# State-space stage of a decoder layer: products with the input issued ahead into two kept PSUM banks

## The chip, the cores and the metric

The kernel runs on one core of one Trainium2 chip. The metric is the device time of one execution in microseconds (us), the median of several runs.

## The reference

One layer of a decoder trunk over 1024 tokens and 1024 channels, in float32. Four token mixers of width 256 (a diagonal complex state-space model, two kinds of attention and RWKV-7 time mixing) read the same projection of the input; their outputs are projected up, gated and summed; then follow an output projection, layer norm, an MLP and a gated embedding. The change lies in the state-space mixer. Cut to that:

```python
# 16 groups of 16 channels, 64 complex states each
bu_re = jnp.einsum('bsgh,gph->bsgp', ug, bb_re)
bu_im = jnp.einsum('bsgh,gph->bsgp', ug, bb_im)
_, _, x_re, x_im = lax.associative_scan(combine, (a_re, a_im, bu_re, bu_im), axis=1)
y = (jnp.einsum('bsgp,ghp->bsgh', x_re, c_re) - jnp.einsum('bsgp,ghp->bsgh', x_im, c_im)
     + d * ug)
y = jax.nn.gelu(y.reshape(bsz, s, BRANCH_WIDTH))
y = y * jax.nn.sigmoid(y @ glu_w + glu_b)
```

## The kernel before

**The whole program.** TensorE (PE) does nearly everything as matmuls of 128x128 weights with 512 columns in a fast float32 format, three for each float32-accurate product. They fill two kinds of PSUM banks: three with the tag `mm` (function `pmm`, line 358) and five with the tag `x` (`px`, line 361).

**Who sets the order.** A planner, the class `Driver` (line 89), runs at build time. Each stage is a Python generator; a `yield 0.1` says "go on 0.1 us after my last result is there", by the planner's own table of costs. While a stage waits, the planner takes the next matmuls of a filler, `merges` (line 1647): up-projections and gates of branches that are already there, called the dense work below. The planner thereby fixes the order of instructions of PE; those of DVE and ACT are chained in the order of the planner's start times. So a different cost or yield in one stage moves instructions in everything that is planned behind it.

**The state-space stage** (`s5`, line 1370) works on 128 chunks of 8 tokens. It has two halves (`p4`), each with four state tiles of 128 states, real and imaginary. A half goes through these steps:

1. PE: products of the input `U` with `GT`, 16 of them, into two `x` banks (lines 1387 to 1392).
2. DVE: rotation by `E` into `Z`, eight scans over the chunks, rotation back into `X`, first the real part (`i` = 0), then the imaginary part (lines 1394 to 1414). The two parts are written by one instruction each.
3. PE: for each of two banks (`g4`) four column blocks (`j`): one product of `U` with `Tg` (what a chunk's own input gives; 128 rows), then one of `X` real and one of `X` imaginary with `Hm` (what the state gives; 64 rows, the lower half for `g4` = 0, the upper for `g4` = 1), added up in the same place (lines 1418 to 1426).
4. ACT and DVE: GELU of each bank into `Y` (lines 1427 to 1433); SP stores `Y` (line 1435).

Behind both halves, the stage loads its result as `yt`, multiplies it with the GLU weights `gw` and stores it. These products are in plain float32: one of them appears in the trace as two passes, that is two weight loads and two MATMUL records. In the text, step 3 of a half is a product block.

Lines 327 and 280 in the trace are those of the helpers that issue every matmul and every other instruction, so groups are told apart by the tiles' names.

Of the kernel before, what the change touches and what calls it, by code (L numbers as in the profile page):

```python
# [16 lines left out]
P = 128  # L17
# [299 lines left out]
def body(ctx, tc, I, O, dbg=None):  # L317
    nc = tc.nc
    drv = Driver()
# [23 lines left out]
    def nm(s):  # L343
        uid[0] += 1
        return f"{s}_{uid[0]}"
# [15 lines left out]
    def px():  # L361
        return ps.tile([P, 512], F32, tag="x", name=nm("x"), bufs=5)
# [907 lines left out]
    def s5_tables(pool):  # L1270
# [93 lines left out]
        for k in range(5, 7):  # L1364
            grow(k)
            yield 0.1
        yield from s5(pool, GT, Tg.rearrange("p g s h -> p g (s h)"), Hm.rearrange("p i a s h -> p i a (s h)"),
                      E.rearrange("p i j a -> p i a j"), U)

    def s5(pool, GT_, Tg_, Hm_, E_, U_):  # L1370
        def tt(o, a, b, op):
            V.tensor_tensor(out=o, in0=a, in1=b, op=op)

        def tq():
            return pool.tile([P, 4, P], F32, tag="s2k", name=nm("tq"), bufs=4)

        gw = pool.tile([P, 2, 256], F32, tag="s2k", name="gw", bufs=4)
        SY.dma_start(out=gw, in_=I["glu_w"].rearrange("(a p) c -> p a c", p=P))
        yield 0.1
        for p4 in range(2):  # L1380
            a4 = slice(p4 * 4, p4 * 4 + 4)
            GT, Hm, Ev = GT_[:, :, a4], Hm_[:, :, a4], E_[:, :, a4]
            Tg, U = Tg_[:, p4 * 8:p4 * 8 + 8], U_[:, p4 * 8:p4 * 8 + 8]
            Z = pool.tile([P, 2, 4, P], F32, tag="t1k", name=nm("Z"), bufs=2)
            X = pool.tile([P, 2, 4, P], F32, tag="t1k", name=nm("X"), bufs=2)
            yield 0.1
            sr, si = px(), px()
            for i, o in ((0, sr), (1, si)):
                for j in range(4):
                    for e in range(2):  # L1390
                        T.matmul(o[e * 64:e * 64 + 64, j * P:(j + 1) * P], lhsT=GT[:, i, j, e * 64:e * 64 + 64],
                                 rhs=U[:, j * 2 + e, :], start=True, stop=True)
            s3r, s3i = (o.rearrange("p (a j) -> p a j", j=P) for o in (sr, si))
            a, b = tq(), tq()
            tt(a, s3r, Ev[:, 0], ALU.mult)
            tt(b, s3i, Ev[:, 1], ALU.mult)
            tt(Z[:, 0], a, b, ALU.add)
            a, b = tq(), tq()
            tt(a, s3i, Ev[:, 0], ALU.mult)
            tt(b, s3r, Ev[:, 1], ALU.mult)  # L1400
            tt(Z[:, 1], a, b, ALU.subtract)
            for i in range(2):
                for j in range(4):
                    pr = p4 * 4 + j
                    V.tensor_tensor_scan(out=Z[:, i, j, :], data0=s5k[:, pr:pr + 1].to_broadcast([P, P]),
                                         data1=Z[:, i, j, :], initial=0.0, op0=ALU.mult, op1=ALU.add)
            z3 = [Z[:, i, :, 0:127] for i in range(2)]
            e3 = [Ev[:, i, :, 0:127] for i in range(2)]
            for i in range(2):
                G.memset(X[:, i, :, 0:1], 0.0)  # L1410
                a, b = tq()[:, :, 0:127], tq()[:, :, 0:127]
                tt(a, e3[0], z3[i], ALU.mult)
                tt(b, e3[1], z3[1 - i], ALU.mult)
                tt(X[:, i, :, 1:128], a, b, ALU.subtract if i == 0 else ALU.add)
            Y = pool.tile([P, 8, P], F32, tag="t1k", name=nm("Y"), bufs=2)
            Ye = Y.rearrange("p (a e) c -> p e a c", e=2)
            yield 0.1
            for g4 in range(2):
                o = px()
                for j in range(4):  # L1420
                    g = j * 2 + g4
                    pr, es = g // 2, slice((g % 2) * 64, (g % 2) * 64 + 64)
                    os_ = o[:, j * P:(j + 1) * P]
                    T.matmul(os_, lhsT=Tg[:, g], rhs=U[:, g, :], start=True, stop=False)
                    for i in range(2):
                        T.matmul(os_, lhsT=Hm[es, i, pr], rhs=X[es, i, pr, :], start=False, stop=i == 1)
                w = pool.tile([P, 512], F32, tag="s2k", name=nm("gl"), bufs=4)
                A.activation(out=w, in_=o, func=AF.Square)
                V.tensor_scalar(out=w, in0=w, scalar1=0.044715, scalar2=1.0, op0=ALU.mult, op1=ALU.add)
                tt(w, o, w, ALU.mult)  # L1430
                A.activation(out=w, in_=w, func=AF.Tanh, scale=math.sqrt(2.0 / math.pi))
                V.scalar_tensor_tensor(out=Ye[:, g4], in0=w.rearrange("p (a b) -> p a b", b=P), scalar=1.0,
                                       in1=o.rearrange("p (a b) -> p a b", b=P), op0=ALU.add, op1=ALU.mult)
            for s in range(8):
                SY.dma_start(out=SCR["y"].rearrange("(g h) s c -> s h g c", h=16)[s, :, p4 * 8:p4 * 8 + 8],
                                  in_=Y[s * 16:(s + 1) * 16])
        yt = []
        for i, tg in enumerate(("Tg", "GT")):
            y_ = pool.tile([P, 1024], F32, tag=tg, name=nm("yt"), bufs=1)
            SY.dma_start(out=y_, in_=SCR["y"][i * P:(i + 1) * P].rearrange("p s c -> p (s c)"))  # L1440
            yt.append(y_)
        yield 0.1
        for ct in range(2):
            for h in range(2):
                hs = slice(h * 512, (h + 1) * 512)
                o = px()
                for kt in range(2):
                    T.matmul(o, lhsT=gw[:, kt, ct * P:(ct + 1) * P], rhs=yt[kt][:, hs], start=kt == 0, stop=kt == 1)
                th = pool.tile([P, 512], F32, tag="s2k", name=nm("gl"), bufs=4)
                A.activation(out=th, in_=o, func=AF.Tanh, scale=0.25, bias=s5k[:, 8 + ct:9 + ct])  # L1450
                yf = pool.tile([P, 512], F32, tag="s2k", name=nm("yf"), bufs=4)
                V.scalar_tensor_tensor(out=yf, in0=th, scalar=1.0, in1=yt[ct][:, hs], op0=ALU.add, op1=ALU.mult)
                if h == 0:
                    ynat = pool.tile([P, 1024], F32, tag="a", name=nm("ynat"), bufs=1)
                A.activation(out=ynat.rearrange("p (c s) -> p c s", s=8)[:, :, h * 4:h * 4 + 4],
                             in_=yf.rearrange("p (s c) -> p c s", s=4), func=AF.Copy, scale=0.25)
            SY.dma_start(out=SCR["Y"][0, ct], in_=ynat)
        yield 0.1
        finished["s5"] = True
# [41 lines left out]
    for n in MERGES:  # L1501
        g = MERGES.index(n)
# [748 lines left out]
```

## Time and profile before

| | |
|---|---|
| median of 3 runs | 1860.12 us (1857.07 to 1865.44) |
| the profiled execution | 1853.48 us, span 1851.7 us |
| PE busy | 1802.2 us, 97% of the span |
| DVE busy | 1238.8 us, 67% |
| ACT busy | 715.7 us, 39% |
| POOL busy | 206.7 us, 11% |
| mean granted clock of PE | 0.99 |
| the state-space stage's products | 661.4 to 741 us |

A busy PE is not one at its peak: matmuls overlap, a record's duration is longer than the distance between starts, and at the lower clock PE is busy all the time too. What a step costs on PE is therefore read from the distance of starts, and from the granted clock of a stretch (1.00 is 2.4 GHz, 0.50 is 1.2 GHz).

### The profile page before, as it was taken

How to read it: one execution, taken by the hardware profiler on the slowest of the kernel's cores; microseconds unless marked ns; L12 is line 12 of the kernel's file. 1: busy time of each engine (PE TensorE's matmuls, PEld its weight loads, DVE VectorE, ACT ScalarE, POOL GpSimd, SP SyncE). 2: the span in 40 equal slices, each digit the busy share in tenths (PEclk: the TensorE clock that was granted, in tenths of full speed). 3: DMA queues.
4: the chain of work that ended last, by engine and by line, in shares of the span. 5: the costliest groups of instructions: out<-in, count | busy, mean ns of one | idle time of the engine just before them, and what ended most of it. 6: DMA issues, size and time to landing. Idle time of an engine off the chain costs nothing.

```text
span 1851.7 us, 27604 instructions
## 1 busy us (share of the span) xinstructions
PE 1802.2 (97%) x9651; PEld 1469.5 (79%) x9651; DVE 1238.8 (67%) x2596; ACT 715.7 (39%) x1412; POOL 206.7 (11%) x279
## 2 busy tenths in 40 slices
PE   8999999998999999999999999999999999999998
PEld 7877777777888877777877887788888887888876
DVE  8675855615876665688867667666656666866574
ACT  5443343224554312555544116343333344443230
POOL 0331111110000000000000001111111211122000
PEclk9999999999999989999999999999999999999999
DMA  7344222224432412412154128898888899988441
GB/s 256 106 125 111 75 85 91 69 74 131 139 108 74 101 40 61 141 55 64 45 197 164 53 68 237 243 254 224 250 247 242 212 289 266 281 226 222 127 148 46
DMA packets 178013, 275.27 MB, mean 149 GB/s; under 512 B 37825, under 2 KB 59617, under 8 KB 177745
## 3 DMA queue, kind: packets, MB, share of 16 engines
q1 hardware_dynamic: 155552, 226.31, 37.6%
q0 software_dynamic: 22320, 47.18, 12.9%
q8 instruction: 76, 1.25, 0.3%
q14 instruction: 65, 0.52, 0.1%
HBM read 199.76 MB, written 56.89 MB: 139 GB/s over the span
## 4 chain that ended last, share of the span: by engine, by line
PE 59%; DVE 7%; DMA 3%; ACT 2%; issue 1%; SPq 0%; DVEq 0%; ACTq 0%; POOLq 0%
PE mm L327 29%; PE x L327 29%; DVE R L280 2%; PE x L332 2%; DMA wr<-in_mlp_w2t_dram 1%; DVE W L280 1%; DVE tq L280 1%; DVE sn L280 1%; DMA scr_g<-gs 1%; DMA wl<-in_mlp_w_dram 0%; DVE Z L280 0%; DMA wr<-wl 0%; SPq L280 0%; ACT W L280 0%; ACT R L280 0%
## 5 line engine op out<-in xcount | busy, mean ns | idle before, releaser
L327 PE MATMUL mm<-t,wh 128*128 128x512 f32 x1600 | 511.3, 401 | 2.7 <-ACT th L280 1.4
L327 PEld LDWEIGHTS mm<-t,wh 128*128 128x128 f32 x1600 | 291.8, 189 | 64.4 <-issue 3.8
L327 PE MATMUL mm<-t,wl 128*128 128x512 f32 x800 | 313.5, 392 | 0.4 <-DVE wl L280 0.4
L327 PE MATMUL x<-t,wp 128*128 128x512 f32 x1152 | 267.5, 392 | 6.8 <-ACT wp L280 4.4
L327 PEld LDWEIGHTS x<-t,wp 128*128 128x128 f32 x1152 | 217.5, 189 | 54.2 <-ACT wp L280 5.2
L327 PE MATMUL x<-sx,wp 128*128 128x512 f32 x768 | 179.6, 389 | 0.3 <-DVE wp L280 0.3
L327 PEld LDWEIGHTS mm<-t,wl 128*128 128x128 f32 x800 | 150.8, 189 | 33.8 <-DVE wl L280 0.9
L327 PEld LDWEIGHTS x<-sx,wp 128*128 128x128 f32 x768 | 144.1, 188 | 30.6 <-DVE wp L280 0.7
L280 ACT CAST wh<-wr 128x512 fp32r<-128x512 f32 (+1 forms) x125 | 74.5, 596 | 123.4 <-PE mm L327 92.4
L280 ACT CAST wp<-wr 128x512 fp32r<-128x512 f32 x96 | 59.0, 620 | 143.0 <-DMA wr<-wl 68.7
L280 DVE TENSOR_TENSOR wp<-wr,wp 128x512 fp32r<-128x512 f32 x96 | 65.7, 688 | 71.2 <-ACT wp L280 71.1
L280 POOL TENSOR_TENSOR wl<-wr,wh 128x512 fp32r<-128x512 f32 x50 | 67.4, 1349 | 280.5 <-ACT wh L280 280.3
L327 PE MATMUL mm<-t,wp 128*128 128x512 f32 x384 | 90.2, 390 | 0.0
L327 PE MATMUL mm<-sx,wp 128*128 128x512 f32 x384 | 89.9, 389 | 0.1
L327 PE MATMUL mm<-wo,t 128*128 128x512 f32 x384 | 89.0, 391 | 0.0
L327 PEld LDWEIGHTS mm<-t,wp 128*128 128x128 f32 x384 | 71.9, 188 | 15.7 <-DVE wp L280 0.9
L327 PEld LDWEIGHTS mm<-sx,wp 128*128 128x128 f32 x384 | 72.0, 188 | 15.4 <-DVE sx L280 0.5
L327 PEld LDWEIGHTS mm<-wo,t 128*128 128x128 f32 x384 | 71.6, 188 | 14.5
L280 DVE TENSOR_TENSOR wp<-wl,wp 128x512 fp32r<-128x512 f32 x64 | 43.8, 688 | 42.9 <-ACT wp L280 42.9
L280 DVE TENSOR_TENSOR wl<-wr,wh 128x512 fp32r<-128x512 f32 (+1 forms) x75 | 47.4, 634 | 35.8 <-ACT wh L280 32.9
L280 DVE TENSOR_TENSOR wp<-wh,wp 128x512 fp32r<-128x512 f32 x64 | 43.9, 689 | 29.5 <-ACT wp L280 29.5
L280 ACT CAST wp<-wl 128x512 fp32r<-128x512 f32 x64 | 39.3, 620 | 53.7 <-PE x L327 26.2
(379 smaller groups left out, 3188.1 us busy)
## 6 DMA issues: line engine op xcount, KB each, us to landing
wr<-in_w_in_dram SPq DMA_DIRECT2D x110, 256.0 KB
scr_H<-sn SPq DMA_DIRECT2D x100, 256.0 KB
wr<-in_mlp_w_dram SPq DMA_DIRECT2D x84, 256.0 KB
sn<-scr_H SPq DMA_DIRECT2D x84, 256.0 KB
wh<-in_mlp_w_dram SPq DMA_DIRECT2D x56, 256.0 KB
wl<-in_mlp_w_dram SPq DMA_DIRECT2D x56, 256.0 KB
wr<-wl POOLq DMA_DIRECT2D x32, 256.0 KB, 6.2
wl<-wr POOLq DMA_DIRECT2D x32, 256.0 KB, 4.4
```

Of the source, the lines that this page charges most:

```text
L280: r = f(*a, **kw)
L327: return nc.tensor.matmul(out, lhsT=lhsT, rhs=rhs, **kw)
L332: return nc.tensor.transpose(out, in_, idn)
```

## The change

The `Tg` products move ahead of the step that turns `Z` into `X`: two `x` banks are taken there, eight products are issued into them, and the banks are marked as held for the planner until their last product. Then come the products with `X` real for both banks, a `yield 0.1`, and those with `X` imaginary, each bank followed by its GELU. Since the four column blocks of a bank are now open at the same time, only the first product of a bank carries the start flag.

```diff
+            o2 = [px(), px()]
+
+            def product(g4, j, i):
+                g = j * 2 + g4
+                pr, es = g // 2, slice((g % 2) * 64, (g % 2) * 64 + 64)
+                ab = (Tg[:, g], U[:, g, :]) if i < 0 else (Hm[es, i, pr], X[es, i, pr, :])
+                T.matmul(o2[g4][:, j * P:(j + 1) * P], lhsT=ab[0], rhs=ab[1], start=i < 0 and j == 0, stop=i == 1,
+                         skip_group_check=j > 0)
+            for g4 in range(2):
+                drv.held.add(o2[g4].name)
+                for j in range(4):
+                    product(g4, j, -1)
             z3 = [Z[:, i, :, 0:127] for i in range(2)]
...
             yield 0.1
             for g4 in range(2):
-                o = px()
                 for j in range(4):
-                    g = j * 2 + g4
-                    pr, es = g // 2, slice((g % 2) * 64, (g % 2) * 64 + 64)
-                    os_ = o[:, j * P:(j + 1) * P]
-                    T.matmul(os_, lhsT=Tg[:, g], rhs=U[:, g, :], start=True, stop=False)
-                    for i in range(2):
-                        T.matmul(os_, lhsT=Hm[es, i, pr], rhs=X[es, i, pr, :], start=False, stop=i == 1)
+                    product(g4, j, 0)
+            yield 0.1
+            for g4 in range(2):
+                o = o2[g4]
+                for j in range(4):
+                    product(g4, j, 1)
+                drv.held.discard(o.name)
                 w = pool.tile([P, 512], F32, tag="s2k", name=nm("gl"), bufs=4)
```

PE's order in the first product block before (`x_7263` and `x_7282` are the two banks, `mm_...` is dense work; in the program each bank has four such pairs of rows):

```order
L327 MATMUL mm_7256<-y_6597,vl_7123 128x512
L327 MATMUL x_7263<-U,Tg 128x128
L327 MATMUL x_7263<-X_7147,Hm 128x128 x2
...
L327 MATMUL x_7282<-U,Tg 128x128
L327 MATMUL x_7282<-X_7147,Hm 128x128 x2
...
L327 MATMUL mm_7325<-t_107,wh_7128 128x512
```

48 dense matmuls stand between the products with `GT` and this block.

PE's order of the same half in the change (the banks are now `x_7187` and `x_7188`):

```order
L327 MATMUL x_7151<-U,GT 64x128 x8
L327 MATMUL x_7152<-U,GT 64x128 x8
L327 MATMUL x_7187<-U,Tg 128x128 x4
L327 MATMUL x_7188<-U,Tg 128x128 x4
L327 MATMUL mm_7136<-t_115,wh_7084 128x512
...
L327 MATMUL mm_7257<-y_6571,vl_7123 128x512
L327 MATMUL x_7187<-X_7147,Hm 128x128 x4
L327 MATMUL x_7188<-X_7147,Hm 128x128 x4
L327 MATMUL x_7187<-X_7147,Hm 128x128 x4
L327 MATMUL x_7188<-X_7147,Hm 128x128 x4
L327 MATMUL mm_7257<-y_6597,vh_7122 128x512
```

The `Tg` products have moved right behind `GT`; then 39 dense matmuls (12, 24 and 3) follow and then all 16 `Hm` products, real part first, with no dense work between the two parts. Behind them stand 24 dense matmuls, the second half's `GT` and `Tg`, 39 dense ones (9, 24 and 6) and its `Hm` products.

DVE's order between the first half's imaginary part of `X` and the second half's first rotation, in the change:

```order
L280 TENSOR_TENSOR X_7147<-tq_7204,tq_7205 128x4x127
L280 TENSOR_TENSOR wl_7238<-wr_7030,wh_7237 128x512
L280 TENSOR_SCALAR gl_7273<-gl_7273 128x512
L280 TENSOR_TENSOR gl_7273<-x_7187,gl_7273 128x512
L280 TENSOR_SCALAR gl_7283<-gl_7283 128x512
L280 SCALAR_TENSOR_TENSOR Y_7209<-gl_7273,x_7187 128x4x128
L280 TENSOR_TENSOR gl_7283<-x_7188,gl_7283 128x512
L280 SCALAR_TENSOR_TENSOR th_7222<-th_7222,mm_7257 128x512
L280 SCALAR_TENSOR_TENSOR Y_7209<-gl_7283,x_7188 128x4x128
...
L280 SCALAR_TENSOR_TENSOR th_7255<-th_7255,mm_7304 128x512
...
L280 TENSOR_TENSOR tq_7359<-x_7341,E 128x512
```

Both GELUs (`gl`, `Y`) are now interleaved; before, the first bank's three instructions stood ahead of the second's. The number of instructions in between is the same, 13.

Further on, the planner's times differ and so does the order of the second attention: behind its last product with the values, 39 dense matmuls (27 and 12) stand before the next gate, where there were 15 (3 and 12). On SP the first load of `yt` stands ahead of three loads of weights that it stood behind.

## Rows read from the trace of the kernel before

**Rows 1.** The page, part 1: engine, busy time, share of the span, instructions.

```profile
PE 1802.2 (97%) x9651; PEld 1469.5 (79%) x9651; DVE 1238.8 (67%) x2596; ACT 715.7 (39%) x1412; POOL 206.7 (11%) x279
```

**Rows 2.** Windows around the state-space stage, by engine, with granted clock and DMA share.

```profile
core 0: us, PE busy (x) PEld busy (x) DVE busy (x) ACT busy (x) POOL busy (x), PEclk, DMA share, GB/s
674.30:679.00 4.70, 3.35 (x20) 2.43 (x18) 3.89 (x6) 0.00 (x0) 0.00 (x0) 1.00 0.10 28
679.00:688.30 9.30, 9.30 (x31) 7.07 (x30) 1.81 (x3) 1.23 (x2) 0.00 (x0) 0.50 0.00 0
688.30:692.40 4.10, 4.10 (x11) 3.21 (x11) 2.88 (x6) 2.04 (x4) 0.00 (x0) 0.50 0.16 47
...
707.50:717.50 10.00, 8.60 (x49) 6.50 (x48) 8.00 (x13) 1.23 (x2) 0.00 (x0) 1.00 0.21 66
```

**Rows 3.** Timeline, first product block: start, us, engine, instruction [idle before <-releaser].

```profile
672.92 0.69 DVE L280 TENSOR_TENSOR X<-tq,tq 128x508 f32<-128x508 f32 x1
...
674.34 0.38 PE L327 MATMUL x<-U,Tg 128*128 128x128 f32 x2
...
675.65 0.69 DVE L280 TENSOR_TENSOR X<-tq,tq 128x508 f32<-128x508 f32 x1
...
676.48 0.46 PE L327 MATMUL x<-X,Hm 64*128 64x128 f32 x2 [1.35 <-DVE X L280]
...
677.29 0.71 PE L327 MATMUL x<-X,Hm 64*128 64x128 f32 x4
...
677.92 0.49 PE L327 MATMUL x<-U,Tg 128*128 128x128 f32 x2
...
678.34 0.71 PE L327 MATMUL x<-X,Hm 64*128 64x128 f32 x4
```

**Rows 4.** Timeline, second product block: the gap, and one bank's square and product to Y.

```profile
709.76 0.46 PE L327 MATMUL x<-X,Hm 64*128 64x128 f32 x2 [1.40 <-DVE X L280]
...
713.42 0.60 ACT L280 ACTIVATE gl<-x 128x512 f32<-128x512 f32 x1 [6.27 <-PE x L327]
...
715.97 0.69 DVE L280 SCALAR_TENSOR_TENSOR Y<-gl,x 128x512 f32<-128x512 f32 x1 [0.70 <-ACT gl L280]
```

**Rows 5.** PE timeline elsewhere: 260-column passes, alternating 64-row products, products with GT.

```profile
66.18 0.28 PE L327 MATMUL x<-vl,t 128*128 128x260 f32 x1
...
66.53 0.28 PE L327 MATMUL x<-vl,t 128*128 128x260 f32 x1
...
93.11 2.82 PE L327 MATMUL x<-AR,BK 64*128 64x128 f32 x32
...
661.42 1.97 PE L327 MATMUL x<-U,GT 128*64 128x128 f32 x32
...
663.32 0.73 PE L327 MATMUL mm<-t,wh 128*128 128x512 f32 x2
```

**Rows 6.** Windows where the state-space tables are made; columns as in rows 2.

```profile
624.40:627.80 3.40, 3.40 (x32) 3.36 (x32) 0.63 (x2) 0.00 (x0) 0.00 (x0) 1.00 0.00 0
627.80:631.30 3.50, 3.50 (x20) 3.50 (x19) 3.03 (x4) 1.62 (x3) 0.00 (x0) 0.51 0.11 37
```

**Rows 7.** Timeline, dense matmuls, every third one: full clock, then half clock.

```profile
701.89 0.39 PE L327 MATMUL mm<-t,wl 128*128 128x512 f32 x1
...
702.57 0.39 PE L327 MATMUL mm<-t,wl 128*128 128x512 f32 x1
...
689.34 0.63 PE L327 MATMUL mm<-t,wl 128*128 128x512 f32 x1
...
690.62 0.63 PE L327 MATMUL mm<-t,wl 128*128 128x512 f32 x1
```

**Rows 8.** Windows of the second attention and what follows; columns as in rows 2.

```profile
740.00:960.00 220.00, 210.24 (x1319) 171.96 (x1317) 167.30 (x283) 117.73 (x271) 6.67 (x39) 1.00 0.30 98
960.00:1000.00 40.00, 37.51 (x163) 30.48 (x164) 34.77 (x56) 18.61 (x35) 0.00 (x0) 1.00 0.49 152
```

**Rows 9.** PE timeline: products of the stage's output with the GLU weights.

```profile
734.00 7.03 PE L327 MATMUL x<-yt,gw 128*128 128x512 f32 x16
```

## The prediction

> **What bounds the kernel now.** I began with the page. PE is busy for 97% of the span [rows 1], so what counts is time on PE: passes that take longer than they must, gaps, and stretches at the lower clock. A transfer or a DVE step counts only where PE waits for it.
>
> Next come the windows around the state-space stage [rows 2], and in them its two product blocks, one per group of four state tiles. The first lasts from 674.3 to 688.3, 14.0 us, the second from 707.5 to 717.5, 10.0 us, for the same instructions. The reader is to see the clock column: 1.00 at the start of the first block, 0.50 (the level of 1.2 GHz) from 679.0 through its end and 4.1 us into the dense work behind it, 1.00 in all of the second block.
>
> The timeline of the first block [rows 3] shows two losses. PE issues the first `Tg` product at 674.34, when the real part of X is there (672.92 plus 0.69 is 673.61), but the imaginary part is written from 675.65 to 676.34; the second `Hm` product waits for it, 1.35 us idle. And the eight groups (one `Tg` product over 128 rows, two `Hm` products over 64) alternate: a `Tg` product, two passes, takes 677.92 to 678.34, 0.42 us; two `Hm` products, four passes, take 677.29 to 677.92, 0.63 us, 0.158 a pass. The second block has the same gap, 1.40 us [rows 4].
>
> **The change, part by part.** No instruction is added or removed: per block 8 `Tg` products (16 passes) and 16 `Hm` products (32 passes). They move on PE.
>
> *The gap.* In the new order PE goes from `GT` to the eight `Tg` products, then through 12+24+3 dense matmuls, then to `Hm` for the real part in both banks, then for the imaginary part. Dense matmuls cost 0.227 us each (three in 0.68 us) [rows 7], so 39 cost 8.85. With 1.95 us for `Tg` (below) PE reaches the first `Hm` 10.8 us after `GT`. `GT` ends at 663.32 [rows 5], so that is 674.1: X's real part is there at 673.61, 0.5 us earlier. The real part's 16 passes take 2.53 us, to 676.65; the imaginary part is there at 676.34. The gap of 1.35 us goes, and of 1.40 in the second block, with margins of 0.5 and 0.3 us.
>
> *The `Tg` products side by side.* What 16 such passes cost in a row the trace does not show. From above: 0.21 each, as between `Hm` products, 3.36 us. From below: passes over all 128 rows with 260 columns, back to back, take 0.117 each (three in 0.35 us) [rows 5]. I take 0.122, 1.95 us, near the lower end: a plain float32 pass of 128 columns streams about as long as one of 256 in the dense format, and these rows too change weights at every pass without leaving the 128-row shape.
>
> Here a rule speaks against the change. The Trainium skill (TensorE: Matmul & The Clock Gate, "Measured speedup vs the span model") says that a weight load overlaps matmuls in flight only where its row group differs. By it the `Tg` passes, all on the same rows, would take about what an `Hm` pass takes, 16 x 0.158 = 2.53 us, and each block would give back 0.6 us less. The row of the 260-column passes speaks against it: they share their rows and are too quick for a load of their own between them.
>
> *The `Hm` products side by side.* In the new order four products of one bank, all on one half of the rows, follow each other, as the pairs do now: 32 x 0.158 = 5.06 us. The lower end is 0.088, where 64-row products alternate between the halves (32 passes in 2.82 us) [rows 5]; only three places in a block alternate, so I stay at 0.158.
>
> *Changes of shape.* Two `Tg` passes amid `Hm` take 0.42 instead of 0.24 us: 0.18 for two changes, 0.09 each. Each block keeps two around `Hm`, 0.18 us; the one behind `GT` exists already.
>
> Sum of a block at full clock: 1.95+5.06+0.18 = 7.2 us against 10.0, a gain of 2.8 (1.4 with `Tg` at 0.21; 5.0 with `Hm` at 0.088). Both blocks: 5.6 us.
>
> *The clock.* Block one lost 14.0-10.0 = 4.0 us against block two, and the 4.1 us of dense work behind it ran at 1.28 us for three against 0.68 [rows 7], 1.9 us lost: 5.9 in all. The fall came 2.5 us after the gap of 1.35 us, with the alternating products in between. Without the gap, and with 10 us of thinly used PE cut into pieces of 1.95 and 5.1 us between dense work, I take it that the clock stays: bounds 0 and 5.9, and I choose 5.9.
>
> *Other engines.* The two kept banks make four of five `x` banks live. Block two's second `Tg` bank is one whose GELU must be over: in block two now, square to `Y` takes 713.42 to 716.66, 3.2 us [rows 4], and in the new order 24 dense matmuls (5.4 us) and `GT` (1.9) lie in between, so it is covered. DVE runs the GELUs of both banks interleaved, 13 instructions between the last X and block two's first `tq`. The first bank is done at about 677.9 and its square at 678.6; twelve instructions of some 0.6 us behind that, as the scale of the rows of X (0.69) and of `Y` (0.69) has it, end near 686.3, and `GT`'s first bank is full at 685.9. That uses up most of the margin of 0.5 us there and opens no gap worth counting. On SP the first `yt` load, which reuses `Tg`'s buffer, moves ahead of three weight loads; `Tg` is released earlier, so nothing queues behind it. POOL only clears one column of X.
>
> *Downstream.* From the end of the stage the planner lays out the second attention differently. There PE is idle for 9.8 us in 740 to 960 and 2.5 in 960 to 1000 [rows 8]. The dense work is the same, only cut otherwise; I count zero, with bounds of -5 and +12.
>
> **Sum:** 5.6+5.9 = 11.5 us less. The profiled execution took 1853.48 us (span 1851.7); the sum gives 1842.0 there. It lies 6.6 us under the median of the three runs, 1860.12, about as much as one more fall of the clock would cost, so runs with two falls may be usual; that I don't know, and I take the 11.5 us from the median: **1848.6 us**.
>
> **Rivals.** *(a) The blocks shrink, the clock falls all the same.* For it: at 627.8 it fell after 32 passes with no gap at all and stayed at 0.51 for 3.5 us [rows 6], so a long run of thin passes is enough, and 5.1 us of `Hm` alone is a longer one; and the same gap cost block two no fall. Against: block two's 7.7 us of the same products behind its gap ran at 1.00. With the old loss the time is 1860.1-5.6 = 1854.5; with two falls as short as that at 627.8 (about 1.7 us lost each) 1852. The Trainium skill (TensorE: Matmul & The Clock Gate, "Why this matters for your kernels") warns only of idle gaps longer than these; by it removing 1.35 us would bring no clock back, and this rival's 1854.5 would be the result. The trace bears it out in part: block two kept its clock.
>
> *(b) The gain is lost in the second attention.* The planner's order leaves 39 dense matmuls between the last attention product and the next branch, where 15 were: 24 fewer (5.4 us) to cover its waits. If PE waits that much more, 1854; if its 12.3 us of idle doubles, 1861.
>
> *(c) Slower: a new wait for X's real part.* Where the old order had 48 dense matmuls before X was needed, now 39 and the `Tg` products stand. If DVE starts a block's chain more than 0.5 us later than in block one now, PE stands before `Hm` with both banks held. With twice the present gap, 2.8 us, in each block, and the clock falling in both, where it now falls in one: -5.6+5.6+5.9 = +5.9, 1866. Against it: neither margin above is negative.
>
> *(d) The change does only half of what it says.* Both parts of X are issued before the first yield, so the planner waits for both: its order has no dense work between the two sets of `Hm`. That is in the sum; it costs nothing so long as both are there.
>
> **Chances.** Forecast 0.50, (a) 0.27, (b) 0.15, (c) 0.08. The forecast's own range is 1843 (5 us of idle gone downstream) to 1852. Range of all: down to 1841 (`Hm` partly at 0.088), up to 1860, which takes in (a) and nearly all of (b). A difference of 0.5% (9.3 us) is about what a measurement can tell from none. Faster by more takes most of the forecast and little else: 0.47; same 0.45; slower 0.08.
>
> **What would show it.** Right: no idle row before `Hm` by DVE X; `Tg` passes at about 0.12 and `Hm` at 0.16 us; 1.00 in the clock column from 640 to 740; the first `yt,gw` product of the stage some 11 us earlier than at 734.00 [rows 9], give or take the six matmuls by which the planner shifts it. Wrong: `Tg` at 0.21; 0.50 anywhere in the stage; a wait of `Hm` on the real part; more than 12 us of idle PE in the 260 us behind the stage.

## The result, and the profile after

The change made the kernel **0.7% faster** by the ratio of its runs to those of before, 0.9931 with a 95% interval of 0.9909 to 0.9952. The medians, 1850.51 us (1847.46 to 1856.31, 5 runs) against 1860.16 us (1857.07 to 1865.44, 5 runs) before, lie 9.65 us or 0.5% apart, inside that interval. Forecast were 1848.6 us and a range of 1841 to 1860. The profiled execution is the run of 1850.51 us, span 1848.7 us; it can be set beside the median as it is.

The page, part 1, of the kernel after (engine, busy time, share of the span, instructions; before: [rows 1]):

```profile
PE 1797.1 (97%) x9651; PEld 1467.7 (79%) x9651; DVE 1237.6 (67%) x2596; ACT 715.4 (39%) x1412; POOL 206.0 (11%) x279
```

PE is as full as before, so the gain must be cheaper work or a higher clock, and not idle time removed. The timeline of the stage after shows where (start, us, engine, instruction, [idle before <-releaser]; before: [rows 3 to 5, 9]):

```profile
664.01 1.97 PE L327 MATMUL x<-U,GT 128*64 128x128 f32 x32
...
665.91 2.05 PE L327 MATMUL x<-U,Tg 128*128 128x128 f32 x16
...
675.46 0.69 DVE L280 TENSOR_TENSOR X<-tq,tq 128x508 f32<-128x508 f32 x1
...
676.77 1.71 PE L327 MATMUL x<-X,Hm 64*128 64x128 f32 x16
...
678.19 0.69 DVE L280 TENSOR_TENSOR X<-tq,tq 128x508 f32<-128x508 f32 x1
...
679.02 1.68 PE L327 MATMUL x<-X,Hm 64*128 64x128 f32 x16 [0.55 <-DVE X L280]
680.63 0.74 PE L327 MATMUL mm<-y,vh 128*128 128x512 f32 x2
...
686.34 1.97 PE L327 MATMUL x<-U,GT 128*64 128x128 f32 x32
...
698.56 0.69 DVE L280 TENSOR_TENSOR X<-tq,tq 128x508 f32<-128x508 f32 x1
...
699.39 1.68 PE L327 MATMUL x<-X,Hm 64*128 64x128 f32 x16 [0.23 <-DVE X L280]
...
701.24 0.69 DVE L280 TENSOR_TENSOR X<-tq,tq 128x508 f32<-128x508 f32 x1
...
702.08 2.60 PE L327 MATMUL x<-X,Hm 64*128 64x128 f32 x16 [1.00 <-DVE X L280]
704.60 1.22 PE L327 MATMUL mm<-y,vh 128*128 128x512 f32 x2
...
724.66 7.03 PE L327 MATMUL x<-yt,gw 128*128 128x512 f32 x16
```

The products are cheap: 16 `Hm` passes go from 679.02 to 680.63, and the dense matmul behind them starts there. But `Hm` still waits for X, three times, and the set for the imaginary part follows the set for the real part with nothing between them. The last `Hm` row is longer than the others (2.60 against 1.68), because the clock fell. The windows show it (columns as in [rows 2]):

```profile
676.00:682.00 6.00, 5.45 (x42) 4.54 (x41) 4.52 (x8) 1.75 (x3) 0.00 (x0) 1.00 0.07 22
...
699.00:702.00 3.00, 1.84 (x17) 1.52 (x16) 2.97 (x5) 0.00 (x0) 0.00 (x0) 1.00 0.00 0
702.00:705.00 3.00, 2.92 (x17) 2.73 (x18) 1.10 (x3) 0.84 (x2) 0.00 (x0) 0.60 0.14 44
705.00:709.00 4.00, 4.00 (x10) 3.07 (x10) 3.09 (x6) 2.44 (x5) 0.00 (x0) 0.50 0.00 0
...
740.00:960.00 220.00, 209.39 (x1316) 173.15 (x1315) 171.74 (x291) 116.06 (x270) 6.67 (x39) 0.99 0.30 96
960.00:1000.00 40.00, 38.19 (x167) 30.87 (x167) 32.09 (x53) 17.06 (x34) 0.00 (x0) 1.00 0.46 146
```

The first block now keeps the clock (1.00, where [rows 2] had 0.50); the second, which kept it before, loses it.

**A measure for the stage.** The planner puts different numbers of dense matmuls into the stage, so I take the time from the first `GT` product to the first `yt,gw` product less 0.227 us per dense matmul of the program in between [rows 7]. Before: 734.00-661.42-186x0.227 = 30.4 us. After: 724.66-664.01-180x0.227 = 19.8. The stage gained 10.6 us, the median 9.65.

The spans of these two traces differ by only 3.0 us, though (1851.7 and 1848.7). Ahead of the first `GT` product, where the program is the same, the kernel after took 2.6 us longer (664.01 against 661.42), and behind the first `yt,gw` product 5.0 us, less 0.227 per dense matmul. In the 14 traces of all kernels the part ahead takes 658.8 to 664.3 us. So a single pair of traces says what the stage gained, and not what the kernel did.

The measure is called "the stage" below, with 198 dense matmuls in e1, e2, e4, e5 and e10, 174 in e3 and 204 in e7.

### The profile page after: what moved, and what is told of

Its sections match the earlier page's. It is cut to its first block, busy times and chain, and to the rows that moved or that the text cites. A ratio compares the mean times of both kernels' runs of the same rounds, so it can differ in the third digit from the quotient of the medians.

```text
span 1848.7 us, 27601 instructions
## 1 busy us (share of the span) xinstructions
PE 1797.1 (97%) x9651; PEld 1467.7 (79%) x9651; DVE 1237.6 (67%) x2596; ACT 715.4 (39%) x1412; POOL 206.0 (11%) x279
```

## The experiments

They are grouped by question. Ratios are to runs of the kernel before beside them on the same chip; "single" is one profiled run, "again" a second trace of the same kernel. The waits are those inside the product blocks, with the block's number; those of one block are added up, and one ahead of its first `Hm` pass is counted with them.

| order of the products | median us (runs) | ratio to before | stage us | waits inside the blocks |
|---|---|---|---|---|
| before | 1860.16 (5) | | 30.4; again 30.4 | 1: 1.35; 2: 1.40; again the same |
| the change | 1850.51 (5) | 0.9931 (0.9909 to 0.9952) | 19.8; again 16.6 | 1: 0.55, again 0.55; 2: 1.23, again 1.28 |
| e1: ahead, `Hm` later | 1840.5 (6) | 0.9885 (0.9861 to 0.9909) | 13.7 | none |
| e2: grouped, in the old place | 1841.57 (6) | 0.9887 (0.9859 to 0.9915) | 13.6; again 13.6 | none |
| e3: ahead, `Hm` in pairs | 1851.78 (8) | 0.9942 (0.9921 to 0.9962) | 25.9; again 24.5 | 1: 1.76, again 1.77; 2: 2.21, again 2.77 |
| e4: old order, later | 1861.37 (12) | 1.0001 (0.9981 to 1.0021) | 23.9; again 23.8 | none over 0.4 |
| e5: half the changes of shape, later | 1850.53 (12) | 0.9961 (0.9941 to 0.998) | 20.4 | none |
| e7: grouped, halves in turn | 1846.56 (7) | 0.9930 (0.9906 to 0.9954) | 15.2 | none |
| e10: e7 in part, e2's order kept | 1843.79 (6) | 0.9910 (0.9890 to 0.9930) | 13.2 | none |

### Is it the waits, the order, or issuing ahead?

**e1** changes one number of the changed kernel, so that the planner waits longer for X:

```diff
-            yield 0.1
+            yield 2.0
             for g4 in range(2):
                 for j in range(4):
                     product(g4, j, 0)
```

> The changed kernel with the planner told to wait 2.0 us instead of 0.1 before the products with X real, so that some 9 more dense matmuls stand ahead of them. Measure for the stage in all runs: from the first product with GT to the first yt,gw product, less 0.227 us for each dense matmul in between (before: 72.6 - 186 x 0.227 = 30.4; changed: 60.7 - 180 x 0.227 = 19.8). Theory A (what is left of the waits, 0.55 and 1.23 us, and the clock's fall behind them are one thing): no idle row before Hm, the clock 1.00 through the stage, 19.8 - 1.8 - 3.2 = 14.8. Rival B (long thin pieces pull the clock down, gap or not): no idle row, but 0.50 behind an Hm piece in at least one half, about 17 to 18. Device time: A some 4 to 5 us under the changed kernel, B about 2 us.

The PE timeline of e1, its first block:

```profile
673.73 2.82 PE L327 MATMUL x<-X,Hm 64*128 64x128 f32 x32
676.48 0.74 PE L327 MATMUL mm<-t,wh 128*128 128x512 f32 x2
```

All 32 passes run as one row, 2.75 us to the next dense matmul, 0.086 a pass; nothing waits and the clock stays at 1.00 in the stage. The stage falls to 13.7 us.

**e2** issues nothing ahead: it keeps the block in its old place and only groups it.

```diff
-            o2 = [px(), px()]
+            o2 = []
...
-            for g4 in range(2):
-                drv.held.add(o2[g4].name)
-                for j in range(4):
-                    product(g4, j, -1)
...
             yield 0.1
-            for g4 in range(2):
-                for j in range(4):
-                    product(g4, j, 0)
-            yield 0.1
+            o2.extend((px(), px()))
+            for i in (-1, 0):
+                for g4 in range(2):
+                    for j in range(4):
+                        product(g4, j, i)
             for g4 in range(2):
                 o = o2[g4]
                 for j in range(4):
                     product(g4, j, 1)
```

> Nothing is issued ahead: the Tg products stand where they stood before the change, but all eight in a row, then the eight with X real, then the eight with X imaginary. Theory A (a change between 128-row and 64-row products costs about 0.23 us and there were 16 in a block; an Hm pass by itself takes 0.09): Tg 1.8 and Hm 3.0 us in a block of about 5 us, no wait for X imaginary since 3.3 us of products stand before it, and the stage's measure at 15 to 16, as good as with the products ahead. Rival B (what helped is that the Tg products are out of the way before X is there): blocks of 8 us or more and a measure of 22 or more.

```profile
671.73 1.95 PE L327 MATMUL x<-U,Tg 128*128 128x128 f32 x16
673.60 2.82 PE L327 MATMUL x<-X,Hm 64*128 64x128 f32 x32
676.35 0.72 PE L327 MATMUL mm<-t,wh 128*128 128x512 f32 x2
```

In e2's PE timeline a block takes 676.35-671.73 = 4.62 us where the old one took 10.0 [rows 2], and since `Tg` covers the wait for X's imaginary part there is none. Time and stage are those of e1: **grouping gives the gain; issuing ahead adds nothing to it**, and where it brings PE to X earlier it costs waits. A second trace (**e8**, the same kernel) gave 13.6 us of stage and 1840.77 us, single:

> The grouped block in its old place once more, for a second trace. By the theory that the gaps and waits amid the thin products, and the many changes, are what brings the clock down in the stage, it is 1.00 again in both blocks, no wait stands in them, and from the first GT product to the first gw product it takes 58.6 us again. By the theory that the falls come by chance in any thin stretch, one may show here.

**e4** is the old order with the longer wait of e1; **e6** is its second trace. The edit, in the kernel before:

```diff
-            yield 0.1
+            yield 2.0
             for g4 in range(2):
                 o = px()
```

> The kernel before with the planner told to wait 2.0 us instead of 0.1 before its product block: the alternating order stays, the wait for X imaginary goes. Theory A (the gap pulled the clock down): no idle row, blocks of 8.5 us at 1.00, the stage's measure about 22. Rival B (the thin alternating block does it by itself): 0.50 from within a block on, in one half or both, and a measure of 26 to 33. Both: 8 groups of 1.05 us in a block at full clock. Device time by A some 8 us under the kernel before, by B within 3 us of it.

> The old order without its gap once more, for a second trace. Its time was that of the kernel before (ratio 1.000), though its trace, of its fastest run, showed no gap and a clock of 1.00 in both blocks. If other runs of it lose the clock in the stage, as the 2.8 us of saved gaps not being seen in its median would say, this trace shows 0.5 to 0.9 in at least one block or behind it. If it shows 1.00 again, the loss lies outside the stage.

The gaps of 1.35 and 1.40 us are gone, both traces show 1.00 in both blocks, and yet the ratio is 1.0001. The stage's rows name one reason; PE timeline of e4, around the second block:

```profile
707.02 0.50 PE L327 MATMUL mm<-t,wl 128*128 128x512 f32 x1 [2.17 <-DVE wl L280]
...
708.05 0.38 PE L327 MATMUL x<-U,Tg 128*128 128x128 f32 x2
708.37 0.71 PE L327 MATMUL x<-X,Hm 64*128 64x128 f32 x4
709.00 0.49 PE L327 MATMUL x<-U,Tg 128*128 128x128 f32 x2
...
716.40 0.73 PE L327 MATMUL mm<-t,wh 128*128 128x512 f32 x2
```

The wait for X has become one for the weight rest `wl`, which VectorE makes behind its state chain: 2.17 us back out of 2.75. The other part of the answer stays open. By the stage e4 should still gain 6.5 us, from the clock kept in block one. But its traces are of runs with a mean granted clock of 0.992 (1853.77 us) and 0.994 (1848.71 us, the single run), while the median of its twelve timed runs has 0.9885; where those lose the clock no trace shows. Even 0.9885 is more than the 0.985 of the runs of before beside them; that alone should give 6.5 us (0.0035 x 1862), and the medians differ by 2.6 (1863.98 and 1861.37).

### What does a change of shape cost?

**e3** has the `Tg` products ahead as in the change, and then each real and imaginary pair of `Hm` products together; **e9** is its second trace.

```diff
             for g4 in range(2):
-                for j in range(4):
-                    product(g4, j, 0)
-            yield 0.1
-            for g4 in range(2):
                 o = o2[g4]
                 for j in range(4):
-                    product(g4, j, 1)
+                    for i in range(2):
+                        product(g4, j, i)
```

> Tg ahead as in the change, but the Hm products in the old order, X real and X imaginary of one column block directly behind each other. Theory A (the change of shape was the price): Hm passes at 0.09 us, 3.0 us for 32, and the second product waits about 2 us for X imaginary in both halves. Rival B (two products into the same columns directly behind each other wait for one another): Hm passes at 0.16 us, 5.1 us for 32. The wait stands in both, and the clock may fall behind it; the stage's measure is 17 to 24 by A and 4 us more by B.

> The order with the Tg products ahead and the Hm products in pairs once more, for a second trace: waits of 1.7 and 2.2 us for the imaginary part of X after the first two passes of each block. By the theory that such a wait ahead of a run of thin products brings the clock down, it falls behind both blocks again; by chance, in one or in none.

The PE timeline of e9, its first block, at full clock:

```profile
675.37 0.48 PE L327 MATMUL x<-X,Hm 64*128 64x128 f32 x2
677.62 3.24 PE L327 MATMUL x<-X,Hm 64*128 64x128 f32 x30 [1.77 <-DVE X L280]
680.79 0.50 PE L327 MATMUL mm<-y,vh 128*128 128x512 f32 x1
```

30 passes in 3.17 us are 0.106 a pass, far less than the 0.158 that the old order showed between `Tg` products. What made those passes slow was the change of shape on either side. That they take more than e2's 0.086 is no price of adding to the same columns, as the single starts below show. The waits are the longest of all, since X's imaginary part is wanted after two passes.

**e5** has e4's place and wait, and groups by two column blocks, 8 changes of shape per block instead of 16; its edit stands against e2.

```diff
-            yield 0.1
+            yield 2.0
             o2.extend((px(), px()))
-            for i in (-1, 0):
-                for g4 in range(2):
-                    for j in range(4):
-                        product(g4, j, i)
             for g4 in range(2):
                 o = o2[g4]
-                for j in range(4):
-                    product(g4, j, 1)
+                for j in (0, 2):
+                    for i in (-1, 0, 1):
+                        product(g4, j, i)
+                        product(g4, j + 1, i)
```

> The block stays in its old place and begins, as in the two earlier runs, only when both parts of X are there (no gap). Its products come in four groups of two Tg and four Hm products, so that TensorE changes between 128-row and 64-row passes 8 times per block, where the old order has 16 and the grouped block 2. Theory A (a change of shape costs 0.24 us, Tg 0.115 and Hm 0.088 a pass, whatever the order): a group lasts 4 x 0.115 + 8 x 0.088 + 2 x 0.24 = 1.64 us, a block 6.6 us, between the 4.6 of the grouped block and the 8.5 of the old order without its gap. Rival B (as the prediction had it: a change costs 0.09, and an Hm pass behind another of its own half of the rows 0.158): a group lasts 4 x 0.115 + 8 x 0.158 + 2 x 0.09 = 1.9 us, a block 7.6. Rival C (the cost lies in two products on the same columns of a bank in direct succession, which this order no longer has): 4.9 us. The time: between the grouped block's 1841 and the old order's 1860, about 1846 by A with the clock at 1.00 in the stage; if the thin work still brings the clock down in it, 0.50 to 0.90 there and 2 to 6 us more.

PE timeline of e5, first block:

```profile
676.96 0.60 PE L327 MATMUL x<-U,Tg 128*128 128x128 f32 x4
...
680.31 0.71 PE L327 MATMUL x<-U,Tg 128*128 128x128 f32 x4
680.95 1.16 PE L327 MATMUL x<-X,Hm 64*128 64x128 f32 x8
682.04 0.71 PE L327 MATMUL x<-U,Tg 128*128 128x128 f32 x4
...
683.76 0.74 PE L327 MATMUL mm<-t,wh 128*128 128x512 f32 x2
```

A group takes 1.73 us (theory A 1.64, B 1.9, C 1.22) and the block 6.80. The starts of the single passes in the traces of e4 and e5 give the price. Within a shape, `Tg` or `Hm`, one pass starts 0.112 us after another; around a change it is 0.20 us from the start of the last pass to the next, and 0.21 from that one to the one behind it. That is **0.19 us a change**, the same in both orders: 6 x 0.112 + 2 x 0.19 = 1.05 us is e4's group of six passes, 12 x 0.112 + 2 x 0.19 = 1.72 e5's of twelve.

Whole blocks differ by more: 4.62 us with 2 changes (e2), 6.80 with 8 (e5), 8.35 with 16 (e4's second block), which would be 0.36 and 0.27 a change. The rest is a second gain of grouping. Where `Hm` products on one half of the rows are followed directly by products on the other half, passes start in pairs within 7 ns of each other, some 0.34 us saved at each such place (the sum of those starts, against 0.112 a pass). e2 has three of them in a block, e9 one, and e4 and e5 none; elsewhere the starts of e2 and e9 are 0.112 us apart too, also where e9's pair adds to the same columns. Of the 3.7 us between the blocks of e4 and e2, changes of shape are thus 14 x 0.19 = 2.7 and the two halves 1.0.

e5 has the wait for `wl` too, 2.15 us, so its stage is 6.8 us above e2's: 2 x 2.18 plus 2.15 is 6.5. Its ratio lies 0.7% above that of e2, about 14 us; the other half of that isn't in the stage of its trace and stays open.

### Do the two halves of the rows matter?

**e7** is e2 with the `Hm` products of the two banks in turn, each on the other half of the rows than the one ahead.

```diff
-            for i in (-1, 0):
-                for g4 in range(2):
-                    for j in range(4):
-                        product(g4, j, i)
+            for g4 in range(2):
+                for j in range(4):
+                    product(g4, j, -1)
+            for i in range(2):
+                for j in range(4):
+                    for g4 in range(2):
+                        product(g4, j, i)
             for g4 in range(2):
                 o = o2[g4]
-                for j in range(4):
-                    product(g4, j, 1)
```

> The grouped block in its old place, but with the Hm products of the two banks in turn, so that each product is on the other half of the rows than the one ahead of it; nothing else moves. Theory A (an Hm pass at full clock takes 0.088 us, whichever half the pass ahead of it used): 32 passes in 2.8 us, the block again 4.6 us, the time that of the grouped block within 0.3% (about 1841). Rival (weight loads overlap better when the halves alternate): less than 2.6 us for the 32 passes, at most 1.5 us less for the kernel. Rival (two banks written in turn cost something): more than 3.1 us.

PE timeline of e7, first and second block, and VectorE's row of the `wl` between them:

```profile
676.40 2.06 PE L327 MATMUL x<-X,Hm 64*128 64x128 f32 x32
678.38 0.73 PE L327 MATMUL mm<-t,wh 128*128 128x512 f32 x2
...
699.63 0.68 DVE L280 TENSOR_TENSOR wl<-wr,wh 128x512 fp32r<-128x512 f32 x1
...
700.37 0.50 PE L327 MATMUL mm<-t,wl 128*128 128x512 f32 x1 [2.81 <-DVE wl L280]
700.72 1.95 PE L327 MATMUL x<-U,Tg 128*128 128x128 f32 x16
```

Theory A fell: the 32 passes take 1.98 us, 0.062 a pass, where four products on one half after another, with three crossings to the other half, make it 0.086, and passes on one half alone 0.112. The Trainium skill (TensorEngine Tiling (Array Packing), "Key Properties") says that different tiles can load weights and multiply in parallel and that a change of tiling mode drains the engine; the trace agrees with both, at 0.062 against 0.112 us a pass and at 0.19 us a change, figures that this section doesn't give. But "nothing else moves" was wrong too: PE's order shows three dense matmuls ahead of the second `GT` set instead of behind it, and a wait for `wl` of 2.81 us ahead of block two gave the gain back. VectorE makes that `wl` only behind its state chain, at 699.63. In the ratios e7 lies 0.4% above e2, some 8 us; the stage has 1.6 of it, the intervals overlap, and the rest stays open.

**e10** (its edit too against e2) alternates only the real part, which leaves every other instruction of PE and VectorE in e2's order.

```diff
-            for i in (-1, 0):
-                for g4 in range(2):
-                    for j in range(4):
-                        product(g4, j, i)
+            for g4 in range(2):
+                for j in range(4):
+                    product(g4, j, -1)
+            for j in range(4):
+                for g4 in range(2):
+                    product(g4, j, 0)
```

> The grouped block in its old place, with the eight Hm products of X's real part on the two halves of the rows in turn and the eight of the imaginary part by bank, as in the grouped block; unlike the run before it, every other instruction of TensorE and VectorE stands where it stood in the grouped block. Theory A2 (an Hm pass takes 0.062 us where each product is on the other half than the one ahead, 0.088 where four follow each other on one half; what the run with all halves in turn lost, it lost by the planner's other order, whose wait for wl of 2.8 us is seen): the 32 passes take 16 x 0.062 + 16 x 0.088 = 2.4 us instead of 2.75, the block 4.25 us, no wait in the stage, 57.8 to 57.9 us from the first GT product to the first gw product instead of 58.58, and a time of 1840 to 1841 (ratio 0.988). Rival (halves in turn themselves cost time behind the block, by the two banks being full at the same moment): a wait in the stage again, 1845 or more.

PE timeline of e10, first block:

```profile
678.11 2.60 PE L327 MATMUL x<-X,Hm 64*128 64x128 f32 x32
680.64 0.73 PE L327 MATMUL mm<-t,wh 128*128 128x512 f32 x2
```

No wait stands in the stage, which agrees with the planner's order having cost e7 its gain. It isn't shown by e10 alone: its imaginary part goes by bank, so its two banks, unlike e7's, aren't full at the same moment. The 32 passes take 2.53 us (expected 2.4) and the stage 13.2, the shortest of all. The time can't be told from e2's: the intervals overlap, and half a microsecond of stage is less than they resolve.

### What brings the clock down in the stage?

Two further traces, of the kernel before and of the changed one, single runs of 1857.64 and 1842.55 us:

> The kernel before once more, for a second trace. By the theory that a gap inside the alternating products is what brings the clock down, it falls in one or both blocks (0.50 to 0.90 behind 677 or 710), and each gap is 1.3 to 1.4 us again. By the theory that falls in the stage come by chance, it may show none.

> The changed kernel once more, for a second trace: waits of Hm on the two parts of X of 0 to 0.6 us in the first block and 0.2 to 1.1 us in the second, Hm passes at 0.088 us at full clock. By the theory that waits inside the thin products bring the clock down, it falls behind the second block again (0.5 to 0.9) and the stage measure from the first GT product to the first gw product, less 0.227 us per dense matmul, is 17 to 20 us; without a fall it is 14 to 17.

Before again: the same two gaps, and again block one fell and block two didn't. After again: the same waits, and this time no fall in either block; PE timeline, its second block:

```profile
694.69 1.68 PE L327 MATMUL x<-X,Hm 64*128 64x128 f32 x16 [0.28 <-DVE X L280]
697.38 1.68 PE L327 MATMUL x<-X,Hm 64*128 64x128 f32 x16 [1.00 <-DVE X L280]
698.99 0.73 PE L327 MATMUL mm<-y,vh 128*128 128x512 f32 x2
```

With e3 and e9 (falls in three of four blocks, behind waits of 1.76 to 2.77 us) there are 12 traced blocks with a wait of 0.5 us or more inside them, and the clock fell to 0.50 in or behind 6. Of 16 blocks without such a wait (e1, e2, e8, e4, e6, e5, e7, e10) none fell, though 6 of them have the many changes of shape and 4 have a wait of over 2 us shortly ahead. So in the traces of this stage a fall goes with idle time **inside** the thin products, and not with the alternation alone. That the idle time is the cause isn't shown: e4, which removes it, is no faster, and its slower runs have no trace. The fall comes and goes from run to run (the change fell in one of two traces), and elsewhere in the program the clock falls without a gap [rows 6].

## Why the prediction was right, and where its working was not

- **Sum and sign: right.** 11.5 us were forecast, 9.65 measured, and the stage gave 10.6 and 13.8 us in two traces. But the terms erred both ways, and that their sum agrees is luck: without the clock the stage gained about 8 us in both traces, where 5.6 were forecast, and of the clock's 5.9 it kept some 2.7 in the first and all in the second.
- **The `Tg` passes: right.** 16 passes go from 671.73 to 673.60 in e2, 0.117 each (forecast 0.122). The rule that the prediction sets against this price, from the Trainium skill (TensorE: Matmul & The Clock Gate), stands in that page's section "The mechanism", just ahead of the one named. By it a pass would take 0.158; the trace doesn't agree for these passes, all on the same rows.
- **The `Hm` passes: mis-sized,** 0.158 forecast, 0.086 measured (e2), and 0.10 in the change itself (16 passes in 1.61 us, with one crossing between the halves). The step that failed is the reading of the `AR,BK` row [rows 5] as "64-row products alternate between the halves". In the program each of its banks is four products on one half before the next half's turn, just the shape of the new order. The right price, 0.088, was on the page, and was put aside as a lower end.
- **The changes of shape: mis-sized,** 0.09 forecast, 0.19 measured (e4, e5). It is the same error from the other side: the 0.18 us on two `Tg` passes is only half of what two changes cost, and the other half, on the `Hm` passes beside them, was taken for the price of the passes themselves (0.63 us for four). With the 0.088 of the `AR,BK` row the prediction's sum of a block comes to 1.95+2.82+0.18 = 5.0 us; e2's takes 4.62.
- **"The gap goes, with margins of 0.5 and 0.3 us": wrong.** The 0.3 rested on the slow pass: real-part passes of 2.53 us would have reached past 678.88, where the imaginary part is there in block one (678.19+0.69); at 0.10 they were through 0.55 us before PE went on. The 0.5 held in block one (676.77 against 676.15). In block two VectorE had other work in front and began the chain at 688.20, 1.86 us after the first `GT` product, where in block one it began at 665.15, 1.14 after it; so PE waited 0.23 us. The prediction had that work and `GT`'s first bank end at about the same time (686.3 and 685.9); quicker `Hm` passes brought `GT` forward, but not VectorE's work. Waits of 1.8 us in all stand where 2.75 were. And since the planner waits for both parts at once, as rival (d) said, nothing lies between the two sets that could cover them. "It costs nothing so long as both are there" was true; they weren't.
- **The clock: right in block one, wrong in block two.** The forecast 5.9 us came back; in the first trace some 3.2 us were lost again (0.60 over 3 us is 2.4 us at 0.50; with the 4 us behind that 6.4, and half of it is lost), in the second none. Rival (a) is right in part: where some of the wait was left, the clock fell in one trace of two.
- **Downstream zero: right in the second attention, not behind it.** Its idle time is 12.4 us, before 12.3 [rows 8]. But behind the first `yt,gw` product the two traces of the change took 5.0 and 1.5 us longer than those of before, less 0.227 per dense matmul. In the MLP, PE waits for ACT and VectorE about 3.3 us longer than in the first trace of before. The waits of PE there, after:

```profile
PE x L327 <- DVE wp L280: 2.7, 2, 2.4
PE x L327 <- ACT wp L280: 2.7, 2, 2.0
PE mm L327 <- DVE sx L280: 0.6, 1, 0.6
```

(columns: us in total, times, longest). Of these before's first trace has the first row alone, but its second trace also has 1.8 us for ACT's `wp`; this varies from run to run, so the change can't be charged with all of it.
- **Rival (c), a new wait for X's real part:** it appeared with 0.23 us, a tenth of its price.

The best order here is not the change: grouping in the old place gives 1841.6 us. Of its 22.4 us against the runs beside it (median 1863.98), the stage has 16.8 (30.4 to 13.6, the same in both pairs of traces). Of these, 10.7 are gaps and products (9.98 us a block at full clock before, 4.62 after, twice) and about 6 the fall of the clock in block one, which both traces of before have and neither of e2's. The spans of the two pairs differ by 18.3 and 16.9 us. What the medians have beyond the stage, 5.6 us, lies outside it; the runs' mean granted clock, in the median 0.992 against 0.985 (0.007 x 1860 is 13), agrees with part of that being clock too, but where, no trace shows.

## What to carry to other kernels

Put products of one shape beside each other before you try to issue any of them ahead: a change of shape cost 0.19 us here, more than a pass (0.112), and grouping alone gave 1.1% where this change gave 0.7%. Then let products on different halves of the rows follow each other: their passes overlap. When a row serves as the price of a new order, read in the program what order that row itself has. And a product that becomes quicker reaches its input sooner: recompute every margin with the new duration, look for waits inside thin work above all, and count those that the planner's new order makes elsewhere.

## What the runs showed that I had not expected

- 64-row passes on one half of the rows start 0.112 us apart, as 128-row passes do, whether they add to the same columns or not. They come to 0.106 us on average with one crossing to the other half in a block (e9), 0.086 with three (e2), 0.062 with products in turn (e7).
- A wait of over 2 us shortly ahead of a thin block left the clock at 1.00 in 4 of 4 blocks; waits of 0.5 to 2.8 us inside one preceded a fall in 6 of 12.
- Runs of one kernel differ by 16 us: twelve runs of e4 go from 1853.77 us at a mean clock of 0.992 to 1870.18 at 0.983. A single trace, above all of a kernel's fastest run, says little about the clock of its median.
